# Projecting the queries first and weaving attention into the mLSTM heads of a hybrid transformer layer

## The chip, the core and the metric

The kernel runs on one core of one Trainium2 chip. Its time is the device time of one execution in microseconds (us); the time of a kernel is the median of several runs. The engines named below are TensorE (PE in the profile; its weight loads are listed apart, as PEld), VectorE (DVE), ScalarE (ACT), GpSimd (POOL) and SyncE (SP, which issues most DMAs here). TensorE writes its results to PSUM, eight banks of 2 KB on each of 128 partitions.

## What is computed

One layer of a diffusion backbone, for 128 context tokens (`xp`) and 1024 latent tokens (`xs`), model width 1024, all in float32. In the reference, cut to what matters:

```python
def trunk_layer(x, mods, ..., rope, ctx_kv, init_f, init_b):
    sh1, sc1, g1, sh2, sc2, g2 = mods                  # silu(cond) @ w_ada + b_ada
    h = rmsnorm(x, norm1_w) * (1 + sc1) + sh1
    aq, ak, av, mq, mk, mv, mo, mg = split(h @ w_in)   # 512, 128, 128, 4 x 512, 16 columns
    aq, ak = rmsnorm(aq, q_norm_w), rmsnorm(ak, k_norm_w)      # per head of 64
    # latent tokens: rotary on aq and ak, keys and values of the context cache appended
    attn_o = attention(aq, keys, vals)                 # 8 query heads, 2 key heads
    hm, st_f, st_b = mlstm_bidir(mq, mk * 128 ** -0.5, mv, gates(mg), init_f, init_b)
    hm = rmsnorm(hm, mlstm_norm_w) * sigmoid(mo)       # 4 heads of 128
    x = x + g1 * (concat([attn_o, hm]) @ w_out)        # 1024 x 1024
    h2 = rmsnorm(x, norm2_w) * (1 + sc2) + sh2
    gate, up = split(h2 @ w_gu)                        # 2 x 2816 columns
    x = x + g2 * ((silu(gate) * up) @ w_down)
```

A latent token attends to 1024 latent and 128 cached context keys, a context token to the 128 context keys alone. The mLSTM works in chunks of 128 tokens, forwards and backwards, with a 128 x 129 state per head and direction. A last rmsnorm gives `y_prompt` and `y_sample`; the context's keys, values and mLSTM states are outputs too.

## The kernel before

The 1152 tokens are nine **blocks** of 128 (block 0 is the context), and three blocks are a **chunk** (`CB`, `NCH`). Most large products are done to float32 accuracy with operands split in two float32r tiles, a rounded part `hi` and the rest `lo`: each block then needs three TensorE products (hi x hi, hi x lo, lo x hi). `load_piece` (L139) loads 128 x 1024 weights by DMA, casts them to `whi` on ScalarE (L152) and subtracts on GpSimd or VectorE (`sub`, L135) for `wlo`. The products stand in `linear_tok` (L399 to L401, tokens on the partitions), `q_group` (L670 to L672, transposed queries of an mLSTM head, 384 columns), `three_blocks` (L1008 to L1010, the FFN's second product), `out_block` (L1040 to L1042) and `products` (L1189 to L1191, the FFN's first product).

The stages in order of the program:

- *Modulation and norm 1.* `shift1` and `scale1` (L279); `normalise` (L257) squares with an accumulator (L261) and scales the rows; transposed and modulated, they become `hTh` and `hTl` (L317 to L344), six tiles of 128 x 8 x 384 float32r.
- *Keys, values, gates* of all blocks, 272 columns (L415); `evac_kvg` adds the gate bias on VectorE.
- *mLSTM heads* (L791 to L838). `head_project` of head h is woven with `head_mlstm` (the scan) of head h - 1. `weave` (L62) emits the main generator and takes steps from side generators at given rates; `beside` (L780) shares them among several. Beside heads 0 to 2 run `gate_work` (L418) and `ada_rest` (L348, the other modulations, `strip_products` of 512 columns), beside head 3 `k_work` (key norm and rotary). A head's evacuation makes `kt`, `va`, `so` and `kT` for each block (L649 to L663); the scan makes weighted values `wv` (L696), states `cs` (L709), masked scores `sd`, sums `nu` (L758) and outputs `hm` (L768 to L772), and writes one `hm_d` in DRAM (L776).
- *Queries* (L835 to L838 beside scan 3, the rest at L962 beside `key_stacks` and the first steps of `attention(0)`); they go through `q_d` in DRAM.
- *Attention* (L877), a chunk at a time: for each block and head six score products into the three-bank tile `S` (one buffer), the maximum (L920), the exponential (L921), a float16 pair `ph`, `pl` (L924, L925), transposes by DMA (L927, L928), and, for each two heads, value products into `po` (L942, L943), scaled into `oT` (L945 to L949).
- *Output projection.* `prefill` (L1045) does the mLSTM half for all blocks, `attn_out` (L1096) the attention half of a chunk, then `norm2` (L1141). Beside it `attention(1)` begins, and `gate_up_pair` (L1172) does the first two blocks' share of two FFN slices early.
- *FFN* (L1326 to L1369), a chunk at a time, with the attention of the next chunk beside it.

PSUM is first split in two pools of four banks: `wi` (L170) for projections and `mm` for all else; from L868 on `mm` has four, `po` one, `S` three. The emitted order is a first order only: the Tile scheduler (`schedule_with_timeline_sim=True`) places the instructions of each engine by its own estimate of times, and `hot(n)` (`tc.high_priority`) raises the priority of what it wraps. Each engine then works its list in order, and a waiting instruction holds up all behind it on that engine.

## Time and profile before

| | |
|---|---|
| median of 3 runs (lowest to highest) | 1618.56 us (1618.33 to 1621.84) |
| the profiled execution | 1619.03 us |
| its span, first to last instruction | 1617.1 us |
| its mean granted TensorE clock | 0.977 |
| read from and written to HBM | 181.16 MB, 11.69 MB |
| all DMA traffic, mean rate | 232.71 MB, 144 GB/s |

The profile comes from one execution, so sums from its rows are to be compared with that execution's own time. A row of the groups names a line, an engine, an operation and its tiles (out<-in), partitions x elements and type, and the count; behind the bar stand busy time, the mean of one in ns, and the engine's idle time just before these instructions, with what ended most of it. Matmuls are pipelined, so the time of a matmul's row is not the time that it takes from TensorE. The granted clock is the share of full speed that TensorE was allowed. Between 381.6 and 622.6 us, and in the first 52, there are windows at half speed.

### The profile page before, as it was taken

What the parts mean: (1) busy time and instruction counts of PE and PEld (TensorE: products, weight loads), DVE (VectorE), ACT (ScalarE), POOL (GpSimd) and SP (SyncE); (2) the same over time, 40 slices, a digit from 0 to 9 for tenths busy, and PEclk for the clock granted to TensorE, in tenths of its full rate; (3) what the DMA queues carried; (4) which work ended last, traced back from release to release, by engine and by line L of the source; (5) the groups of instructions that cost most, each with busy time, mean ns of one, the idle gap of its engine ahead of it and who ended that gap; (6) DMA issues with size and microseconds to landing.
All of it is one profiled execution on the core that took longest, in us unless ns stands there. A gap on an engine that the chain in (4) does not pass through costs nothing. (4 is left out here: it accounts for less than half of the span.)

```text
span 1617.1 us, 23358 instructions
## 1 busy us (share of the span) xinstructions
PE 1532.5 (95%) x8670; PEld 1366.1 (84%) x8670; DVE 965.3 (60%) x1969; ACT 689.8 (43%) x1193; POOL 618.0 (38%) x392
## 2 busy tenths in 40 slices
PE   6899999899898968999999999999999999999996
PEld 2888888898676757998989899898898989999995
DVE  4842363957877668577663646767674474432445
ACT  3522242424534556555643344565552453333322
POOL 1511030413345324443445344444344445544443
PEclk8999999999898988999999999999999999999998
DMA  9244443303155865777773446777684445534441
GB/s 358 67 155 125 117 142 52 82 22 71 50 183 134 180 153 116 174 181 178 180 179 113 148 153 216 188 179 175 156 185 131 131 144 176 151 127 146 144 130 65
DMA packets 386311, 232.71 MB, mean 144 GB/s; under 512 B 169910, under 2 KB 346502, under 8 KB 386198
## 3 DMA queue, kind: packets, MB, share of 16 engines
q1 hardware_dynamic: 384342, 228.04, 52.5%
q10 hardware_dynamic: 1856, 3.19, 0.6%
q8 instruction: 68, 1.11, 0.3%
q14 instruction: 45, 0.37, 0.1%
HBM read 181.16 MB, written 11.69 MB: 119 GB/s over the span
## 5 line engine op out<-in xcount | busy, mean ns | idle before, releaser
L135 POOL TENSOR_TENSOR wlo<-raw,whi 128x1024 fp32r<-128x1024 f32 (+1 forms) x159 | 390.2, 2459 | 512.3 <-ACT whi L152 474.4
L152 ACT CAST whi<-raw 128x1024 fp32r<-128x1024 f32 x239 | 245.0, 1026 | 361.7 <-DMA raw<-in_w_gu_dram 112.8
L1190 PE MATMUL mm<-aTl,whi 128*128 128x384 f32 (+2 forms) x1088 | 363.6, 334 | 0.0
L1189 PE MATMUL mm<-aTh,whi 128*128 128x384 f32 (+2 forms) x1088 | 362.5, 335 | 0.8 <-DVE tn L1217 0.8
L1191 PE MATMUL mm<-aTh,wlo 128*128 128x384 f32 (+2 forms) x1088 | 363.2, 334 | 0.0
L1189 PEld LDWEIGHTS mm<-aTh,whi 128*128 128x128 f32 x1088 | 204.5, 188 | 2.2 <-DVE tn L1217 1.4
L1190 PEld LDWEIGHTS mm<-aTl,whi 128*128 128x128 f32 x1088 | 204.9, 188 | 0.7
L1191 PEld LDWEIGHTS mm<-aTh,wlo 128*128 128x128 f32 x1088 | 204.9, 188 | 0.2
L135 DVE TENSOR_TENSOR wlo<-raw,whi 128x1024 fp32r<-128x1024 f32 (+1 forms) x80 | 98.4, 1230 | 151.7 <-ACT whi L152 147.8
L1008 PE MATMUL mm<-whi,hl 128*128 128x512 f32 x372 | 146.4, 398 | 0.8 <-ACT hl L1221 0.7
L1009 PE MATMUL mm<-wlo,hl 128*128 128x512 f32 x372 | 146.9, 396 | 0.0
L1010 PE MATMUL mm<-whi,hl 128*128 128x512 f32 x372 | 144.3, 396 | 0.8 <-POOL hl L135 0.8
L399 PE MATMUL wi<-whi,hTh 128*128 128x384 f32 (+2 forms) x392 | 135.9, 347 | 5.2 <-ACT hTh L341 5.1
L925 DVE SCALAR_TENSOR_TENSOR pl<-pr,st,ph 128x1152 f16<-128x1152 f32 (+1 forms) x72 | 111.6, 1550 | 47.7 <-ACT ph L924 47.6
L401 PE MATMUL wi<-whi,hTl 128*128 128x384 f32 (+2 forms) x392 | 133.6, 343 | 1.3 <-POOL hTl L135 1.3
L400 PE MATMUL wi<-wlo,hTh 128*128 128x384 f32 (+2 forms) x392 | 133.5, 341 | 0.0
L921 ACT ACTIVATE pr<-S,st 128x1152 f32<-128x1152 f32 (+1 forms) x72 | 81.2, 1128 | 99.7 <-DVE st L920 90.6
L135 POOL TENSOR_TENSOR hl<-tn,hl 128x384 fp32r<-128x384 f32 x66 | 83.5, 1266 | 105.0 <-ACT hl L1221 104.9
L998 DVE TENSOR_TENSOR x<-x,t 128x512 f32<-128x512 f32 x102 | 116.9, 1168 | 0.8
L1217 DVE SCALAR_TENSOR_TENSOR tn<-tn,mm 128x384 f32<-128x384 f32 (+2 forms) x68 | 36.6, 539 | 134.2 <-PE mm L1191 100.4
L918 PE MATMUL S<-kst,qT 128*128 128x384 f32 (+1 forms) x400 | 88.1, 356 | 13.9 <-ACT pr L921 13.8
L920 DVE TENSOR_REDUCE st<-S 128x1 f32<-128x1152 f32 (+1 forms) x72 | 88.8, 1233 | 20.7 <-PE S L918 20.3
(323 smaller groups left out, 2714.2 us busy)
## 6 DMA issues: line engine op xcount, KB each, us to landing
raw<-in_w_gu_dram SPq DMA_DIRECT2D x132, 512.0 KB, 4.0
raw<-in_w_down_dram SPq DMA_DIRECT2D x60, 512.0 KB, 3.6
a<-in_w_ada_dram SPq DMA_DIRECT2D x32, 512.0 KB, 4.2
gl<-g_d SPq DMA_DIRECT2D x36, 256.0 KB, 3.8
aw<-in_w_ada_dram SPq DMA_DIRECT2D x16, 512.0 KB, 8.9
raw<-in_w_in_dram SPq DMA_DIRECT2D x32, 256.0 KB, 5.6
raw<-in_w_out_dram SPq DMA_DIRECT2D x15, 512.0 KB, 4.9
x<-in_x_sample_dram SPq DMA_DIRECT2D x13, 512.0 KB, 6.4
```

What stands on the lines that cost most here:

```text
L135: (dve if eng == "dve" else pool).tensor_tensor(out=out, in0=full, in1=hi, op=ALU.subtract)
L152: nc.scalar.copy(hi[:, :n], raw[:, :n])
L399: mm(ps[:, :n], ah, wh[:, k % 2, c0 : c0 + n], start=(k == 0), stop=False)
L400: mm(ps[:, :n], ah, wl[:, k % 2, c0 : c0 + n], start=False, stop=False)
L401: mm(ps[:, :n], al, wh[:, k % 2, c0 : c0 + n], start=False, stop=(k == KD - 1))
L998: eng.tensor_tensor(out=x1[:, cs], in0=x1[:, cs], in1=t, op=ALU.add)
L1008: mm(ps, ah, wh[:, k % 2, :], start=(k == 0), stop=False)
L1009: mm(ps, ah, wl[:, k % 2, :], start=False, stop=False)
L1010: mm(ps, al, wh[:, k % 2, :], start=False, stop=(k == nk - 1))
L1189: mm(ps, wh[:, k, :], th[:, k, :], start=(k == 0), stop=False)
L1190: mm(ps, wh[:, k, :], tl[:, k, :], start=False, stop=False)
L1191: mm(ps, wl[:, k, :], th[:, k, :], start=False, stop=(k == KD - 1))
```

## The change

- **Float16 pairs for the input projection.** `hT` and the pieces of `w_in` are scaled by powers of two taken from bounds (for `hT` from `scale1` and `shift1`, for weights from the largest absolute value, found on ScalarE by `Abs` with its result thrown into PSUM banks) and split in a float16 `hi` and `lo`; the inverse scale is applied as the results are evacuated. The class `Scaled` does load, scale and pairs. There are still three products for each block.
- **Order.** The queries are projected right after keys, values and gates, with the gate work, the key work and the remaining modulations but one beside them. `attention(0)` is woven into the four heads at a tenth of a step for each unit, with its key stacks and `S` from there on. The last scan has beside it the new `attn_out_first` (the attention half of the output projection for chunk 0, its result written to `x1a_d` in DRAM), the last modulation (gate 5) and the start of `attention(1)`. `hm_d` is three tensors, one a chunk, and the last head writes `hm` in thirds.
- **Engines.** `va` and the first half of `hm` move from VectorE to ScalarE, `so` and (heads 0 to 2) `wv` from VectorE to GpSimd, `so` as two operations.
- **Output projection and FFN.** `gate_up_pair` is gone; `prefill` takes one block at a time, with `norm2` of chunk 0 one block behind.
- **Pools.** Tiles of the projection and of attention lie on the right side. In the heads PSUM has two banks for `wi`, three for `mm` and three for `S`; values use an `mm` bank until the heads are done, then `mm` has four and `po` one.

The core of the diff:

```diff
-QFIRST = [(0, 1), (2,), (3,)]
-QREST = [(4,), (5, 6), (7, 8)]
+SINGLES = [(b,) for b in range(NB)]
...
-    hm_d = drp.tile([TOK, 512], F32, name="hm_d")
+    hm_d = [drp.tile([CT, 512], F32, name=f"hm_d{c}") for c in range(NCH)]
     g_d = drp.tile([2, 2, D], F32, name="g_d")
+    x1a_d = [drp.tile([P, D], F32, name=f"x1a_d{i}") for i in range(CB)]
...
+    def power_scale(tp, one, bound, out):
+        ps = bank()
+        transpose(ps[0:1, 0:P], bound)
+        v = tp.tile([1, 4], F32, name=nm("pv"), tag="pv", bufs=2)
+        dve.tensor_reduce(out=v[:, 0:1], in_=ps[0:1, 0:P], axis=AX.X, op=ALU.max)
+        powers(v, 1)
+        yield
+        ps = bank()
+        mm(ps[:, 0:2], one, v[:, 2:4], start=True, stop=True)
+        dve.tensor_copy(out, ps[:, 0:2])
...
+    class Scaled:
+        def __init__(self, srcs, shape, raws=None):
+            self.srcs, self.shape, self.raws, self.made = srcs, shape, raws, None
+        def ready(self):
+            a, b = self.shape
+            n = self.n = a * b
+            raws = self.raws or [wp.tile([P, 1024], F32, name=nm("iraw"), tag="iraw", bufs=4) for _ in self.srcs]
+            self.raws = raws
+            for raw, src in zip(raws, self.srcs):
+                for part, ap_ in src:
+                    dma(part(raw[:, :n].rearrange("p (a b) -> p a b", b=b)), ap_)
+            yield
+            t = gp.tile([P, 20], F32, name=nm("isc"), tag="isc", bufs=3)
+            for j, raw in enumerate(raws):
+                for i in range(2):
+                    act(bank()[:, 0 : n // 2], raw[:, i * n // 2 : (i + 1) * n // 2], AF.Abs, accum_out=t[:, 12 + 2 * j + i : 13 + 2 * j + i])
+                yield
+            dve.tensor_reduce(out=t[:, 4:5], in_=t[:, 12:20], axis=AX.X, op=ALU.max)
+            dve.tensor_tensor(out=t[:, 4:5], in0=t[:, 4:5], in1=hsc[:, 3:4], op=ALU.mult)
+            yield from power_scale(gp, one1, t[:, 4:5], t[:, 6:8])
+            dve.tensor_tensor(out=t[:, 8:9], in0=t[:, 6:7], in1=hsc[:, 3:4], op=ALU.mult)
+            dve.tensor_scalar(out=t[:, 9:10], in0=t[:, 7:8], scalar1=P ** -0.5, scalar2=None, op0=ALU.mult)
+            dve.tensor_scalar(out=t[:, 10:11], in0=t[:, 7:8], scalar1=0.5, scalar2=None, op0=ALU.mult)
+            self.scale, self.inv, self.inv_k, self.inv_half = t[:, 8:9], t[:, 7:8], t[:, 9:10], t[:, 10:11]
+        def pairs(self, dve_every=2):
+            out = []
+            n, b = self.n, self.shape[1]
+            for j, raw in enumerate(self.raws):
+                w = wp.tile([P, 2, 1024], F16, name=nm("ipair"), tag="ipair", bufs=4)
+                hi, lo = w[:, 0, :n], w[:, 1, :n]
+                if j % dve_every == 0:
+                    act(hi, raw[:, :n], AF.Copy, scale=self.scale)
+                    dve.scalar_tensor_tensor(out=lo, in0=raw[:, :n], scalar=self.scale, in1=hi, op0=ALU.mult, op1=ALU.subtract)
+                else:
+                    act(raw[:, :n], raw[:, :n], AF.Copy, scale=self.scale)
+                    nc.scalar.copy(hi, raw[:, :n])
+                    sub(lo, raw[:, :n], hi, "pool")
+                out.append(tuple(v.rearrange("p (a b) -> p a b", b=b) for v in (hi, lo)))
+            return out
...
+            if b0 < 2 * CB:
+                dve.tensor_scalar(out=xs[b0 + i], in0=xs[b0 + i], scalar1=rs[:, i : i + 1], scalar2=None, op0=ALU.mult)
+            else:
+                act(xs[b0 + i], xs[b0 + i], AF.Copy, scale=rs[:, i : i + 1])
...
-    hTh = [hp.tile([P, KD, CT], F32R, name=f"hTh{c}", tag=f"b{2 * c}") for c in range(NCH)]
-    hTl = [hp.tile([P, KD, CT], F32R, name=f"hTl{c}", tag=f"b{2 * c + 1}") for c in range(NCH)]
+    hp = ctx.enter_context(tc.tile_pool(name="hpk", bufs=1, side="right", reuse_waits="tile"))
+    hT = [hTp.tile([P, 2, KD, CT], F16, name=f"hT{c}", tag=f"hT{c}") for c in range(NCH)]
+    hTh, hTl = [t[:, 0] for t in hT], [t[:, 1] for t in hT]
+    dve.tensor_reduce(out=hs2, in_=shift1, axis=AX.XY, op=ALU.max, apply_absolute_value=True)
+    dve.tensor_reduce(out=hsc[:, 0:1], in_=scale1, axis=AX.XY, op=ALU.max, apply_absolute_value=True)
+    dve.scalar_tensor_tensor(out=hsc[:, 0:1], in0=hsc[:, 0:1], scalar=float(D) ** 0.5, in1=hs2, op0=ALU.mult, op1=ALU.add)
+    powers(hsc, P)
+    for t in (scale1, shift1):
+        dve.tensor_scalar(out=t, in0=t, scalar1=hsc[:, 2:3], scalar2=None, op0=ALU.mult)
...
+            if b == 0:
+                with hot(300):
+                    emit(kvg_steps)
+                    kvg_pairs = kvg.pairs()
+            if b >= 3:
+                for _ in range(3):
+                    next(ada)
+            if b in (3, 4, 5, 6):
+                next(steps)
+            if b == 8:
+                emit(steps)
...
-            dve.tensor_copy(va[:, 0:P], ps[:, P : 2 * P])
+            act(va[:, 0:P], ps[:, P : 2 * P], AF.Copy, scale=w.inv)
             pool.memset(va[:, P : P + 1], 1.0)
             th = mlp.tile([P, P], F32, name=nm("th"), tag="th", bufs=2)
-            act(th, ps[:, 2 * P : 3 * P], AF.Tanh, scale=0.5)
+            act(th, ps[:, 2 * P : 3 * P], AF.Tanh, scale=w.inv_half)
             so = mlp.tile([P, P], F32, name=nm("so"), tag="so", bufs=MB)
-            dve.scalar_tensor_tensor(out=so, in0=th, scalar=1.0, in1=mwh[:, h * P : (h + 1) * P], op0=ALU.add, op1=ALU.mult)
+            pool.tensor_tensor(out=so, in0=th, in1=mwh[:, h * P : (h + 1) * P], op=ALU.mult)
+            pool.tensor_tensor(out=so, in0=so, in1=mwh[:, h * P : (h + 1) * P], op=ALU.add)
...
-        yield from q_group((0, 1))
-        yield from q_group((2,))
-        yield from linear_tok(pieces, P, 3 * P, evac)
+        for c in range(NCH):
+            yield from q_group((c,))
+        for i, _ in enumerate(linear_tok(pieces, P, 3 * P, evac, SINGLES)):
+            if i % 6 == 5:
+                next(nxt_steps, None)
+            yield
+        emit(nxt_steps)
...
-                dve.tensor_scalar(out=wv, in0=blocks[b][2], scalar1=qcol(1, d, b, h), scalar2=None, op0=ALU.mult)
+                if h < NH - 1:
+                    pool.tensor_tensor(out=wv, in0=blocks[b][2], in1=qcol(1, d, b, h).to_broadcast([P, P + 1]), op=ALU.mult)
+                else:
+                    dve.tensor_scalar(out=wv, in0=blocks[b][2], scalar1=qcol(1, d, b, h), scalar2=None, op0=ALU.mult)
...
+        ends = {2: 0, 5: 3, 8: 6} if h == NH - 1 else {8: 0}
...
-            dve.tensor_scalar(out=hm[:, b, :], in0=nu[:, 0, 0:P], scalar1=dn[:, 0:1], scalar2=None, op0=ALU.mult)
+            act(hm[:, b, :], nu[:, 0, 0:P], AF.Copy, scale=dn[:, 0:1])
...
+    w_q = groups_in[0].pairs()
+    steps = groups_in[1].ready()
+    next(steps)
+    weave(linear_tok(w_q, 0, 512, evac_q(qp, qcc, qss, qw)), beside((gates, 0.25), (ada, 0.8), (kwork, 0.8), (steps, 0.3)), 40, 40)
+    emit(steps)
+    groups_in[1].made = groups_in[1].pairs()
+    emit(ada)
+    emit(kwork)
+    es_r.close()
+    es_h.close()
+    es_a.close()
+    es_b.close()
+    ap = ctx.enter_context(tc.tile_pool(name="ap", bufs=1, side="right", reuse_waits="tile"))
+    ap2 = ctx.enter_context(tc.tile_pool(name="ap2", bufs=1, side="right", reuse_waits="tile"))
+    psum["S"] = ctx.enter_context(tc.tile_pool(name="pS", bufs=1, space=PSUM, reuse_waits="tile"))
+    es_d = ExitStack()
+    for name, bufs in (("wi", 2), ("mm", 3)):
+        psum[name] = es_d.enter_context(tc.tile_pool(name="p" + name, bufs=bufs, space=PSUM, reuse_waits="tile"))
...
-                            po = psum["po"].tile([P, 512], F32, name=nm("po"), tag="po")
+                            po = psum["po"].tile([P, 512], F32, name=nm("po"), tag="po") if "po" in psum else bank()
...
+        ahead = load_hm(0)
         load_x1(0)
-        ahead = load_hm(0)
-        order = [(b,) for b in range(NB - 2)] + [tuple(range(NB - 2, NB))]
-        for grp in order:
-            parts = {}
-            for b in grp:
-                load_x1(b + 1)
-                s = b % 6
-                th, tl = (t[:, s // 3 * 4 : s // 3 * 4 + 4, s % 3 * P : (s % 3 + 1) * P] for t in (ath, atl))
-                parts[b] = th, tl
-                hm, ahead = ahead, load_hm(b + 1)
-                ps = bank()
-                for j in range(4):
-                    transpose(ps[:, j * P : (j + 1) * P], hm[:, j * P : (j + 1) * P])
-                psv = ps.rearrange("p (j x) -> p j x", j=4)
-                nc.scalar.copy(th, psv)
-                sub(tl, psv, th.bitcast(F32), "dve")
+        ws = out_pieces(1)
...
+    def attn_out_first(oT, ready):
+        x1 = hTp.tile([P, CB, D], F32, name="x1a", tag="hT0")
+        gt = hTp.tile([P, 6, 512], F32, name="gta", tag="hT1")
+        mx = hTp.tile([P, CB, NQ, P], F32R, name="mxa", tag="hT2")
+        ip = [wp.tile([P, 1024], F32R if i < 2 else F32, name=nm("ip"), tag="ipair", bufs=4) for i in range(4)]
+        ir = [wp.tile([P, 1024], F32R if i < 2 else F32, name=nm("ir"), tag="iraw", bufs=4) for i in range(4)]
+        turn = [0]
...
-    def gate_up_pair(a, fs):
-        a["early"] = []
...
+    oT = []
+    done = set()
+    att = attention(0, oT, done, 200, 100)
+    weave(head_project(0, sts[0]), beside((gates, 0.3), (att, 0.1)), 96, 96)
+    emit(gates)
+    for h in range(1, NH):
+        scan = head_mlstm(h - 1, sts[h - 1])
+        weave(head_project(h, sts[h]), beside((scan, 0.67), (att, 0.11)), 96, 96)
+        emit(scan)
+    scan = head_mlstm(NH - 1, sts[NH - 1])
+    first, ada = attn_out_first(oT, done)
+    oT = []
+    att = chain(att, attention(1, oT, set()))
+    weave(scan, beside((ada, 0.35), (first, 0.25), (att, 0.1)), 57, 57)
+    while len(done) < CB:
+        next(att)
+    emit(first)
+    emit(ada)
+    emit(scan)
+    es1.close()
+    es_wp.close()
+    es_d.close()
+    for name, bufs in (("mm", 4), ("po", 1)):
+        psum[name] = ctx.enter_context(tc.tile_pool(name="q" + name, bufs=bufs, space=PSUM, reuse_waits="tile"))
+    wp = ctx.enter_context(tc.tile_pool(name="wp", bufs=1, reuse_waits="tile"))
+    hp = ctx.enter_context(tc.tile_pool(name="hp", bufs=1, reuse_waits="tile"))
...
+    for _ in prefill(cur, nxt):
+        due += 0.35
         while due >= 1.0:
+            next(att, None)
```

442 lines of the change are left out of this document (211 added, 231 removed).

## The prediction

> **What bounds the kernel now.** I read the page's engine table first, then busy time by stage (the page's slices are too coarse, so I cut the span where TensorE's main products change), then matmul spacing in the timeline, then TensorE's waits in the worst stage.
>
> ```profile
> span 1617.1 us, 23358 instructions
> PE 1532.5 (95%) x8670; PEld 1366.1 (84%) x8670; DVE 965.3 (60%) x1969; ACT 689.8 (43%) x1193; POOL 618.0 (38%) x392
> ```
>
> TensorE (PE) is the bound, but 95% overstates it: a matmul's row lasts longer than its slot. The slot is the distance between starts in a dense stretch, from the timeline:
>
> ```profile
> 1454.74 0.34 PE L1190 MATMUL mm<-aTl,whi 128*128 128x384 f32 x1
> ...
> 1460.98 0.34 PE L1190 MATMUL mm<-aTl,whi 128*128 128x384 f32 x1
> ...
> 881.66 0.39 PE L1010 MATMUL mm<-whi,hl 128*128 128x512 f32 x1
> ...
> 884.45 0.39 PE L1010 MATMUL mm<-whi,hl 128*128 128x512 f32 x1
> ...
> 737.17 0.28 PE L943 MATMUL po<-plT,vs 128*128 128x256 f16 x1
> ...
> 737.83 0.27 PE L943 MATMUL po<-plT,vs 128*128 128x256 f16 x1
> ```
>
> The first two rows are 36 matmuls apart: 6.24 / 36 = 0.173 us for 384 columns of float32r (a row says 0.34). The next two are 12 apart: 0.232 us for 512 columns. The last two are 6 apart: 0.110 us for 256 columns of float16 (0.109 over longer stretches). Count times slot I call TensorE's **work**. By stage (columns: start:end, length, then busy time and instructions of PE, PEld, DVE, ACT, POOL, granted clock, DMA share, GB/s):
>
> ```profile
> 0.00:34.20 34.20, 21.36 (x108) 7.53 (x108) 10.40 (x44) 8.76 (x16) 3.44 (x9) 0.90 0.96 352
> 34.20:81.80 47.60, 40.90 (x280) 38.30 (x281) 42.73 (x114) 28.32 (x65) 27.33 (x22) 0.89 0.35 116
> 81.80:148.80 67.00, 67.00 (x411) 54.25 (x410) 23.09 (x77) 16.46 (x42) 8.69 (x12) 1.00 0.46 139
> 148.80:227.00 78.20, 78.20 (x541) 69.74 (x540) 30.84 (x109) 23.89 (x77) 8.21 (x15) 1.00 0.44 120
> 227.00:308.20 81.20, 78.69 (x523) 70.03 (x523) 52.58 (x175) 25.22 (x90) 20.44 (x31) 1.00 0.35 80
> 308.20:381.60 73.40, 68.72 (x439) 66.16 (x438) 48.70 (x164) 23.57 (x85) 20.27 (x28) 1.00 0.16 44
> 381.60:468.80 87.20, 77.59 (x383) 62.15 (x381) 69.06 (x237) 38.72 (x104) 32.37 (x30) 0.94 0.33 76
> 468.80:622.60 153.80, 124.56 (x603) 99.60 (x603) 114.06 (x214) 81.25 (x124) 57.13 (x35) 0.88 0.69 164
> 622.60:1603.50 980.90, 974.66 (x5393) 897.99 (x5392) 564.42 (x800) 439.44 (x586) 438.91 (x215) 1.00 0.58 156
> 1603.50:1617.10 13.60, 0.80 (x4) 0.32 (x2) 9.46 (x42) 4.22 (x9) 1.26 (x1) 0.67 0.31 116
> ```
>
> They are: loads and first modulations; k/v/gates projection (DVE busy 42.7 of 47.6, so VectorE sets it); heads 0 to 3; queries beside scan 3; attention of chunk 0 with the output projection; FFN; tail. The stage 468.8 to 622.6, worked out:
>
> ```profile
> L1040 PE MATMUL mm<-whi,aTh 128*128 128x512 f32 x72 | 30.0, 420 | 2.5 <-ACT aTh L1076 1.5 <-DVE rv L125 0.9
> L918 PE MATMUL S<-kst,qT 128*128 128x384 f32 x114 | 29.7, 406 | 11.5 <-ACT pr L921 11.5
> L942 PE MATMUL po<-phT,vs 128*128 128x256 f16 x75 | 20.1, 300 | 11.3 <-DVE oT L947 4.8 <-DMA phT<-ph 4.5 <-ACT whi L152 1.6
> ```
>
> Out products (L1040 to L1042 with all their operands) 268 x 0.232 = 62; scores 114 x 0.173 + 10 small = 20; values (L942, L943) 150 x 0.109 = 16; transposes and rest 9: 108 us of work in 153.8. 46 us are lost, partly in waits (the row of L918: scores wait for the exponential of the head before, since the S tile has one buffer), partly because the granted clock was 0.88 (0.12 x 153.8 = 18 us). The same sum for the other stages gives, as work in time: 13 in 34, 36 in 48, 58 in 67, 71 in 78, 73 in 81, 66 in 73, 69 in 87, FFN and tail 971 in 994. In all 1465 of 1617: **152 us are slack**, 65 of it in the two stages from 381.6 to 622.6. There the change can win.
>
> **The change part by part.**
>
> *Float16 pairs.* Three products per block stay three; only the slot shrinks. No row has a 384-column float16 matmul; 256 columns in 0.109 us is 2.35 columns a ns, so I take 0.1635, 0.218 and 0.116 us for 384, 512 and 272 columns, against 0.173, 0.232 and 0.126 (bounds: no gain, and twice this gain, should some ns of the 0.109 be a fixed cost of a matmul). 1152 x 0.0095 + 216 x 0.014 + 216 x 0.010 = 16.1 us off the work.
>
> ```profile
> L399 PEld LDWEIGHTS wi<-whi,hTh 128*128 128x128 f32 x392 | 75.0, 191 | 12.7 <-ACT hTh L341 5.8 <-issue 4.6 <-ACT th L656 0.4
> L942 PEld LDWEIGHTS <-vs 128*128 128x128 f16 x292 | 29.1, 100 | 26.0 <-issue 9.5 <-DVE oT L947 6.1 <-DMA phT<-ph 5.9
> ```
>
> Weight loads fall from 191 to 100 ns. They run beside the products (a 191 ns load fits into a 173 ns slot only so), hence I count nothing for them. The Trainium skill, page "TensorE: Matmul & The Clock Gate", section "Part 3: Packing small matmuls", says otherwise: a weight load overlaps running matmuls only where the row group differs, and these loads take all rows. By that rule 1584 x 0.091 = 144 us would go (an estimate); it is the last rival, and the 0.173 us slot speaks against it.
>
> *FFN without the early pair.* 96 products of 256 columns and 96 of 128 become 96 of 384.
>
> ```profile
> 645.54 0.28 PE L1189 MATMUL mm<-aTh,whi 128*128 128x128 f32 x1
> ...
> 646.54 0.27 PE L1190 MATMUL mm<-aTl,whi 128*128 128x128 f32 x1
> ```
>
> Nine slots, so 128 columns take 0.111. 256 lie between that and 0.173; I take 0.118, the float16 slot plus a little: 96 x (0.118 + 0.111 - 0.173) = 5.4 us off (bounds 4.7 and 10.7). *Scaling.* Six scale chains add 12 small matmuls at 0.11: 1.3 us. Work: 1465 - 16.1 - 5.4 + 1.3, some **1445 us**.
>
> *Other engines.* In the instruction order of the changed kernel, up to the first FFN product:
>
> ```profile
> L261 ACT ACTIVATE jk<-x 128x1024 bf16<-128x1024 f32 x9 | 9.5, 1056 | 1.4 <-DMA x<-in_x_sample_dram 0.9 <-DMA x<-in_x_prompt_dram 0.2
> L261 ACT ACTIVATION_READ_ACCUMULATOR jk<-x 128x1 f32 x9 | 1.7, 190 | 0.0
> L921 ACT ACTIVATE pr<-S,st 128x1152 f32<-128x1152 f32 x64 | 78.3, 1223 | 90.2 <-DVE st L920 86.0 <-DVE rv L125 2.1 <-DVE pl L925 1.8
> L920 DVE TENSOR_REDUCE st<-S 128x1 f32<-128x1152 f32 x64 | 86.5, 1351 | 17.9 <-PE S L918 17.5
> L925 DVE SCALAR_TENSOR_TENSOR pl<-pr,st,ph 128x1152 f16<-128x1152 f32 x64 | 105.3, 1645 | 47.1 <-ACT ph L924 47.0
> L658 DVE SCALAR_TENSOR_TENSOR so<-th,mwh 128x128 f32<-128x128 f32 x36 | 11.8, 330 | 10.6 <-POOL hm L772 9.7 <-ACT th L656 0.3
> L696 DVE TENSOR_SCALAR wv<-va,QT 128x129 f32<-128x129 f32 x64 | 25.9, 409 | 37.7 <-PE mm L705 36.5 <-issue 0.9
> L772 POOL TENSOR_TENSOR hm<-hm,so 128x128 f32<-128x128 f32 x36 | 17.3, 482 | 57.3 <-ACT jkh L771 54.1 <-issue 2.2 <-POOL va L654 1.0
> ```
>
> ScalarE gains 48 absolute-value passes (half of 1.06 us, plus 0.19 for the accumulator, 0.7 each: 34 us), ten casts more for the pairs (10), 36 `va` and 36 `hm` evacuations (0.33 each, 24) and nine attention heads (1.22 for the exponential, as much for the copy and 0.19: 24): 92 more, some 340 in all. VectorE gives away 108 operations like `so` and 48 `wv`: 108 x 0.33 + 48 x 0.41 = 55 us, but takes twelve halves of pairs (1.3 each), nine attention heads (1.35 + 1.65 each) and the scale chains: 420, as before. POOL gains 120 products at 0.48: 240. None comes near 600, so these engines bound single stages only.
>
> *By stage of the new order* (work counted from that order; time is my estimate):
>
> - Loads to first k/v/gates product: 14 of work. The scale of `hT` hangs a dozen VectorE operations of 0.15 us behind `scale1`: 36 (was 34).
> - k/v/gates: 40. VectorE was busy 10.4 + 42.7 = 53 us up to the end of this stage; the new order puts 15 us more ahead of the last gate evacuation (scale chains, three more subtractions, nine modulation units, pieces of the k work). It was saturated, so 12 of them are paid: 60 (was 48).
> - Queries with gates, k work, modulation: 57 of work, 62 of VectorE: 64.
> - Heads 0, 1, 2: 51, 72, 72. Heads 0 to 3 ran at 87 to 90%; VectorE has 27, 50, 45 us there and ScalarE 35 to 50, so there is room for one attention head every 9 us, whose chain of scores, maximum and exponential (1.04 + 1.35 + 1.22 + 0.19) needs 3.8. I keep 90%: 57, 80, 81.
> - Head 3 and the last scan, with the first out products, gate 5 and the start of attention 1: 85 at 90% is 95, then 42 in 57: there VectorE has 60, and the scan's tail was the slow part of stage 381.6 to 468.8 (69 in 87).
> - Other half of the output projection, norm2 and more of attention 1: 70 in 82, with some 6 us until the first w_out pieces are there, since they take the place of tiles that the first half still reads.
>
> Sum: 36 + 60 + 64 + 57 + 80 + 81 + 152 + 82 = **612** against 622.6, though 504 of work stand before the first FFN product instead of 494: nine attention heads of chunk 1 have moved ahead of it. FFN and tail: 1445 - 504 = 941 of work and 21 of slack (23 before, less a little, since chunk 0's FFN has fewer attention heads beside it), **962**. Span 1574; the profiled execution takes 1619.03 for a span of 1617.1, 1.9 more, and the median, 1618.56, is 0.5 below it. So **1575 us**.
>
> **Rivals.**
>
> - *Better fill.* Attention fills the scans' gaps as it does in the FFN (971 in 994, 97%). Heads and scans: 322 / 0.97 = 332 instead of 370: **1537**. For it: the FFN does it with the same attention beside it. Against: in heads 0 and 1 TensorE's row shows no gap (78.20 of 78.20), yet its work is 90% of that; slots beside other kinds of product are longer, and attention adds more of these.
> - *Float16 isn't faster.* Slots stay 0.173 and 0.232, so 1575 + 16: **1591**. Only values at 256 columns speak for the gain.
> - *Slower: PSUM banks.* In the heads `mm` has three banks instead of four, projections two instead of four, and `mm` now also takes the values (18 products, 2.0 us, and their evacuation), query transposes and eight scratch outputs of the absolute value per head. TensorE issues in order, so one late bank holds all.
>
> ```profile
> L758 DVE TENSOR_TENSOR nu<-mm,it 128x258 f32<-128x258 f32 x32 | 13.4, 420 | 10.4 <-PE mm L755 9.7 <-ACT it L751 0.7
> L947 DVE SCALAR_TENSOR_TENSOR oT<-po,vsc,ol 64x128 f32<-64x128 f32 x72 | 24.5, 341 | 14.7 <-ACT ol L945 13.1
> ```
>
> If each of the 27 scan banks of a head waits for one evacuation of 0.42, each scratch 0.7 and each of five value tiles three evacuations of 0.34, that is 11 + 6 + 5 = 22 us a head, 88 in all; less the 18 that the 90% holds already, **1645**. It turns the result from 11 us a head on (1619).
> - *Loads don't overlap*: 1575 + 16 - 144 = **1447**, if all of it shows.
>
> **How the numbers follow.** My stages 0.45 (1555 to 1600); better fill 0.22; float16 no faster, or slower stages yet still a gain, 0.14; PSUM banks 0.14; within 0.2% of before 0.03 (about what a measurement can tell from no change); loads 0.02. The range 1530 to 1620 leaves out most of the bank case and the loads. Faster 0.83, same 0.03, slower 0.14.
>
> **What would show it.** Right: projection slots near 0.1635 us; last k/v/gates product near 96, queries done near 160, first FFN product near 612; clock 1.00 in the heads; FFN and tail near 962. Wrong: waits of projections for ScalarE or of `mm` products for `isc` and `ol` in the heads (banks); slots of 0.173; VectorE idle while TensorE waits before 160.

## The result, and the profile after

The changed kernel takes **1624.6 us** (median of 20 runs, 1618.87 to 1628.66), the kernel before, run beside it, 1619.61 (20 runs). The ratio is 1.0026, with a 95% interval of 1.0016 to 1.0037: slower by a quarter of a per cent, where 1575 us were forecast. The profiled execution took 1626.38 us. Its page, first lines:

```profile
span 1624.6 us, 23438 instructions
...
PE 1507.5 (93%) x8592; PEld 1254.6 (77%) x8592; DVE 937.6 (58%) x1895; ACT 755.6 (47%) x1373; POOL 657.5 (40%) x507
```

Busy time by stage, cut at the same products as before (same columns as in the prediction): loads; keys, values and gates; queries; heads 0, 1, 2; head 3 up to the first out product; the rest of the last scan; output projection and norm 2; FFN; tail.

```profile
0.00:40.00 40.00, 22.95 (x111) 8.72 (x112) 13.31 (x67) 13.86 (x36) 2.56 (x9) 0.84 0.97 355
40.00:93.70 53.70, 47.63 (x384) 32.92 (x384) 42.45 (x138) 36.17 (x84) 19.52 (x18) 0.90 0.59 186
93.70:170.30 76.60, 65.44 (x368) 30.02 (x368) 57.67 (x161) 39.10 (x67) 31.70 (x23) 0.96 0.50 150
170.30:228.50 58.20, 54.70 (x328) 33.74 (x326) 33.37 (x108) 26.95 (x78) 19.73 (x32) 0.94 0.17 49
228.50:309.50 81.00, 75.05 (x490) 54.00 (x489) 48.35 (x119) 54.11 (x143) 25.89 (x48) 1.00 0.36 74
309.50:387.70 78.20, 74.93 (x511) 54.19 (x509) 41.63 (x119) 45.04 (x133) 26.00 (x54) 1.00 0.40 68
387.70:494.50 106.80, 94.42 (x628) 69.38 (x628) 65.18 (x170) 54.43 (x146) 40.01 (x70) 0.92 0.53 116
494.50:547.00 52.50, 44.62 (x255) 34.63 (x254) 42.90 (x110) 29.07 (x71) 14.39 (x14) 0.97 0.53 135
547.00:653.70 106.70, 82.40 (x407) 65.56 (x406) 62.54 (x144) 47.81 (x76) 43.53 (x31) 0.90 0.59 159
653.70:1611.10 957.40, 944.97 (x5123) 871.42 (x5122) 520.89 (x725) 404.82 (x536) 432.95 (x211) 1.00 0.58 156
1611.10:1624.60 13.50, 0.38 (x2) 0.00 (x0) 9.28 (x42) 4.22 (x9) 1.26 (x1) 0.61 0.30 117
```

Set against the forecast, with TensorE's work (count times slot, small products by the distance of their own rows, one count for all kernels from here on; slack is length less work):

| part | forecast | measured | work | slack |
|---|---|---|---|---|
| loads | 36 | 40.0 | 9 | 31 |
| keys, values, gates | 60 | 53.7 | 38 | 15 |
| queries | 64 | 76.6 | 56 | 21 |
| heads 0, 1, 2 | 57, 80, 81 | 58.2, 81.0, 78.2 | 194 | 23 |
| head 3 and last scan | 152 | 159.3 | 122 | 37 |
| up to the first FFN product | 82 | 106.7 | 73 | 33 |
| FFN and tail | 962 | 970.9 | 939 | 32 |

By this count the work fell from 1453 to 1432 us, 21 less (forecast: 20). The slack rose from 164 to 193, where I let it fall by 23. Before the first FFN product it went from 138 to 161 us, and the FFN with its tail added 6.

### The profile page after: what moved, and what is told of

The parts are those of the page before. It is cut to its first block, busy times and chain, and to the rows that moved or that the text cites. A ratio compares the mean times of both kernels' runs of the same rounds, so it can differ in the third digit from the quotient of the medians.

```text
span 1624.6 us, 23438 instructions
## 1 busy us (share of the span) xinstructions
PE 1507.5 (93%) x8592; PEld 1254.6 (77%) x8592; DVE 937.6 (58%) x1895; ACT 755.6 (47%) x1373; POOL 657.5 (40%) x507
## 3 DMA queue, kind: packets, MB, share of 16 engines
q1 hardware_dynamic: 385110, 231.84, 53.7%
## 5 line engine op out<-in xcount | busy, mean ns | idle before, releaser
L136 POOL TENSOR_TENSOR wlo<-raw,whi 128x1024 fp32r<-128x1024 f32 (+1 forms) x144 | 352.0, 2448 | 419.3 <-ACT whi L153 387.9
L153 ACT CAST whi<-raw 128x1024 fp32r<-128x1024 f32 (+1 forms) x216 | 221.6, 1026 | 403.9 <-DMA raw<-in_w_gu_dram 160.4
L1305 PE MATMUL mm<-aTl,whi 128*128 128x384 f32 x1056 | 355.1, 336 | 0.0
L1304 PE MATMUL mm<-aTh,whi 128*128 128x384 f32 x1056 | 354.0, 336 | 0.9 <-DVE tn L1323 0.9
L1306 PE MATMUL mm<-aTh,wlo 128*128 128x384 f32 x1056 | 354.6, 336 | 0.0
L1306 PEld LDWEIGHTS mm<-aTh,wlo 128*128 128x128 f32 x1056 | 198.4, 188 | 1.5 <-issue 1.3
L136 DVE TENSOR_TENSOR wlo<-raw,whi 128x1024 fp32r<-128x1024 f32 (+1 forms) x72 | 85.9, 1193 | 157.0 <-ACT whi L153 156.8
L514 PE MATMUL wi<-ipair,hT 128*128 128x384 f16 (+2 forms) x432 | 142.6, 332 | 9.8 <-ACT ipair L217 3.6
L515 PE MATMUL wi<-ipair,hT 128*128 128x384 f16 (+2 forms) x432 | 143.4, 332 | 4.3 <-DVE ipair L218 4.3
L516 PE MATMUL wi<-ipair,hT 128*128 128x384 f16 (+2 forms) x432 | 143.3, 332 | 0.2 <-POOL hT L136 0.2
L1323 DVE SCALAR_TENSOR_TENSOR tn<-tn,mm 128x384 f32<-128x384 f32 x66 | 36.4, 551 | 134.5 <-PE mm L1306 95.6
L1030 ACT ACTIVATE ph<-pr,st 128x1152 f16<-128x1152 f32 (+1 forms) x72 | 83.8, 1164 | 28.0 <-issue 8.1
```

Source lines behind the costliest of these rows:

```text
L136: (dve if eng == "dve" else pool).tensor_tensor(out=out, in0=full, in1=hi, op=ALU.subtract)
L153: nc.scalar.copy(hi[:, :n], raw[:, :n])
L514: mm(ps[:, :n], ah, wh[:, k % 2, c0 : c0 + n], start=(k == 0), stop=False)
L515: mm(ps[:, :n], ah, wl[:, k % 2, c0 : c0 + n], start=False, stop=False)
L516: mm(ps[:, :n], al, wh[:, k % 2, c0 : c0 + n], start=False, stop=(k == KD - 1))
L1304: mm(ps, wh[:, k, :], th[:, k, :], start=(k == 0), stop=False)
```

## The experiments

Theory after the result: the smaller slots are a gain, and the new order and the scaling give it back in waits, at the queries and around the last scan. Rival: the heads lose it, to PSUM banks shared with attention. Each ratio is to the kernel before, run on the same chip (the changed kernel: 1.0026). A ratio is that of medians, while stages and waits are read from one execution of each kernel; the executions of the changed kernel alone spread over 10 us, so a few us between the stages of two kernels prove little. The code is shortened.

### The float16 pairs alone (f16_alone)

The kernel before, with `hT` and the pieces of `w_in` in float16, unscaled:

```diff
-hi = wp.tile([P, 1024], F32R, ...); hTh = hp.tile([P, KD, CT], F32R, ...)
+hi = wp.tile([P, 2048], F16, ...);  hTh = hp.tile([P, 2, KD, CT], F16, ...)[:, 0]
```

> The kernel before with one part of the change alone: hT and the pieces of w_in as float16 pairs (hi and lo, without the scaling), order, pools and engines as before. The slots of the changed kernel (0.1625, 0.216, 0.116 us for 384, 512, 272 columns) give 18 us less work than before. Theory (the smaller slots are a gain, and the new order gives it back): 1599 to 1606 us, ratio 0.988 to 0.992. Rival (the slots gain nothing where other engines set the pace, so the new order is neutral): within 4 us of before, ratio 0.998 to 1.002.

Measured: 1611.29 us, ratio 0.9957 (0.9942 to 0.9972), less than the theory's gain. The first FFN product starts at 605.0 us instead of 622.6: the whole 17.6 are there. The FFN and tail then take 1004.5 instead of 994.5 for the same work of 969. TensorE's longest waits from the first FFN product on, before and then in this run (sum, times, longest):

```profile
PE S L918 <- ACT pr L921: 1.7, 1, 1.7
PE po L942 <- DMA phT<-ph: 1.1, 2, 0.8
```

```profile
PE po L943 <- DMA phT<-ph: 3.5, 3, 2.6
PE po L944 <- DMA plT<-pl: 1.6, 1, 1.6
```

Value products wait for transposed probabilities 5.1 us instead of 1.3. The pairs gain what their slots say, and 10 of the 17.6 us are lost in the FFN, whose code is the same. These waits are 4 of the 10; the rest is spread over smaller ones and not taken apart.

### The scaling (fixed, nopass, abs_sbuf, abs_dve)

In `fixed` a constant takes the place of the weights' bound; `nopass` leaves out only the passes; `abs_sbuf` moves their thrown-away result; `abs_dve` moves the passes to VectorE:

```diff
-act(bank()[:, 0 : n // 2], raw[...], AF.Abs, accum_out=t[...])   # and maximum, transpose, powers, broadcast
+dve.memset(t[:, 4:5], 2.0 ** -6); powers(t[:, 4:8], P)                          # fixed
+dve.memset(t[:, 12:20], 0.125)                                   # nopass, the chain stays
+act(gp.tile([P, 512], BF16, ...), raw[...], AF.Abs, accum_out=t[...])           # abs_sbuf
+dve.tensor_reduce(out=t[:, 12 + j : 13 + j], in_=raw[:, :n], op=ALU.max, ...)   # abs_dve
```

> The changed kernel with a constant bound for the weights' scales: the absolute-value passes on ScalarE (with their PSUM banks), the maximum, its transpose and its broadcast over partitions are left out. Theory (the scale chains cost a few us at the start and in the queries stage and are hidden in the heads): 4 to 9 us faster than the changed kernel, ratio 0.997 to 1.000. Rival (the chains and the banks that they take hold up every head): 15 us or more faster, ratio at or below 0.993.

> The changed kernel without the absolute-value passes of the weights alone (the partial maxima are constants); the chain behind them (maximum, transpose, powers, broadcast by a product) stays. The constant scale of the run fixed took both away and was 17 us faster than the changed kernel. If the 48 passes on ScalarE and the mm banks that they take are the cost: 10 us or more of the 17 come back, ratio at or below 0.997. If the chain is the cost: within 5 us of the changed kernel, ratio 1.000 to 1.004.

> The changed kernel with the thrown-away result of the absolute-value passes written to one small SBUF tile instead of mm banks. If the banks (eight more per head in a pool of three, TensorE behind them in order) are what the passes cost: 8 us or more faster than the changed kernel, ratio at or below 0.998. If it is ScalarE's time, in order ahead of evacuations: no gain, ratio 1.001 to 1.005.

> The changed kernel with the weights' absolute maximum taken on VectorE (24 reductions of some 1.1 us over whole pieces) instead of 48 passes on ScalarE (37 us by their rows). If ScalarE's order, ahead of evacuations, is what the passes cost: 5 us or more of the 12 that nopass gained come back, ratio 0.996 to 0.9995. If VectorE is as tight in these stages: ratio 1.001 or above.

Measured: fixed 1607.21 us, 0.9932 (0.9910 to 0.9954); nopass 0.9954 (0.9938 to 0.9970); abs_sbuf 1.0011 (0.9993 to 1.0029); abs_dve 0.9993 (0.9978 to 1.0008). Against the changed kernel these are 15, 12, 2 and 5 us less. The passes' rows in the changed kernel:

```profile
L200 ACT ACTIVATE mm<-iraw 128x512 f32<-128x512 f32 x40 | 24.1, 604 | 4.6 <-DVE cs L823 3.8 <-DMA iraw<-in_w_in_dram 0.6
L200 ACT ACTIVATION_READ_ACCUMULATOR mm<-iraw 128x1 f32 x40 | 8.0, 199 | 0.0
L200 ACT ACTIVATE mm<-kraw 128x272 f32<-128x272 f32 x8 | 3.1, 388 | 1.0 <-DMA kraw<-in_w_in_dram 1.0
L200 ACT ACTIVATION_READ_ACCUMULATOR mm<-kraw 128x1 f32 x8 | 1.5, 188 | 0.0
```

That is 37 us of ScalarE, near the 34 that I counted, but I let it cost nothing. A third of it comes out as time, though ScalarE is busy 47% of the span. Of the 12 us, 5 come back when the passes move to VectorE, which frees ScalarE and the banks together; the banks by themselves are worth 2, within what the interval leaves open. That the passes stand in ScalarE's list ahead of evacuations is only argued: TensorE's waits for `th`, the evacuation there, fall from 3.7 us to 2.4 both in nopass and in abs_dve, and all its waits from the first product of keys, values and gates to the first FFN product add up to 74 us in the changed kernel, 70 in nopass and 74 in abs_dve. The scaling costs 15 us in all, close to what the rival of fixed said and far from its theory, and twice the 7 that the pairs alone gained at the end. (The passes add up absolute values, so the scale follows a bound, not the largest value itself, as the part on the change says; only abs_dve takes that.)

What is left when the scaling goes is small. `fixed` and `f16_alone` were run beside the same runs of the kernel before, and take 1607.21 and 1611.29 us: all the rest of the change (order, engines, pools, output projection, no early pair) is worth some 4 us, and the runs of the two overlap. I had put 28 of the 44 us on it.

### The queries' norm (qplain)

```diff
-norm_rope(qp, cc, ss, qr[:, 0:nb], nb, NQ, qw, ...)
```

> The changed kernel without norm and rotary of the queries (left out: they go to attention as projected). Theory (VectorE's chains set the pace of the new queries stage, 74 us from its first to its last product with 56 of work): that stretch shrinks to 60 to 66 us and the whole by 8 to 14 us against the changed kernel, ratio 0.994 to 0.998. Rival (weights, modulation loads and key work set it): under 4 us, ratio 1.000 to 1.004.

This kernel leaves out norm and rotary of the queries, so only its time means anything. Measured: 0.9963 (0.9948 to 0.9978), 10 us less than the changed kernel, as the theory said, but in another place: the stretch from first to last product takes 70.3 us, not 60 to 66. The queries stage of this run:

```profile
92.50:164.60 72.10, 64.41 (x369) 30.01 (x369) 36.29 (x106) 35.92 (x63) 19.60 (x17) 0.95 0.55 169
```

VectorE fell from 57.7 to 36.3 us and the stage only from 76.6 to 72.1; head 0 behind it went from 58.2 to 51.4. So VectorE's norm doesn't set the queries stage alone; it runs over into head 0. Without the absolute-value passes (nopass) the products of this stage took 65.0 from first to last instead of 73.6: so at least two chains keep it at 77, and neither alone.

### Attention in the heads, and the banks (noweave, noweave6, psum32, psum14)

```diff
-weave(head_project(h, sts[h]), beside((scan, 0.67), (att, 0.11)), 96, 96)
+weave(head_project(h, sts[h]), beside((scan, 0.67)), 96, 96)                    # noweave; noweave6 with mm 6, S later
-for name, bufs in (("wi", 2), ("mm", 3)):
+for name, bufs in (("wi", 3), ("mm", 2)):                                       # psum32; psum14: 1 and 4
```

> The changed kernel without attention beside heads 0 to 3 (both rates taken out), so that all of attention 0 stands beside and behind the last scan. Theory (the heads have little slack, attention in them costs its own work, some 2 us a head, but saves the chain of 4 us a head elsewhere): stages of heads 0 to 2 become some 10 to 25 us shorter in sum, the part from the last scan to the first FFN product 30 to 60 longer, ratio 1.015 to 1.03. Rival (PSUM banks shared with attention slow the heads by far more than attention's own work): heads 0 to 2 become over 40 us shorter, ratio at or below 1.002.

> The run noweave (no attention beside the heads) with six mm banks in the heads instead of three: attention's score tile is opened only behind the heads. In noweave the heads 0 to 2 took 50.9, 68.0 and 68.4 us. Bank rival: the scan's products wait for banks, so these three become 15 us or more shorter in sum, ratio at or below 1.046. Theory (three banks are enough without attention's values and transposes): under 8 us shorter, ratio 1.051 to 1.058.

> The changed kernel with three PSUM banks for the projections and two for all else in the heads, instead of two and three. The prediction's bank rival (every scan product, value tile and transpose waits for the evacuation of its bank) makes 20 us or more of losing the third mm bank: ratio 1.015 or above. Theory (the stages of heads 0 to 2 came out at 58, 81 and 78 us, as forecast without bank waits): within 8 us of the changed kernel, ratio 0.998 to 1.008.

> The changed kernel with one bank for the projections and four for all else in the heads. Bank rival: heads faster, ratio at or below 0.996. Theory: no gain from the fourth mm bank; with one projection bank each block's evacuation stands between its products and the next block's, 36 times some 1 us and 12 times 0.5, so slower: ratio 1.01 to 1.03.

Measured: noweave 1710.36 us, 1.0569 (1.0550 to 1.0588), far beyond the theory's range. Heads 0 to 2 took 50.8, 68.0 and 68.4, 30 less in sum, and 20 of these are work that left. But from head 3 on to the first FFN product 384 us pass instead of 266. TensorE's longest waits there:

```profile
PE mm L1048 <- DMA phT<-ph: 33.7, 9, 8.0
PE S L1024 <- ACT pr L1027: 27.3, 10, 3.7
```

With nothing beside it an attention head waits for its exponential and for its transposes; the granted clock was 0.68 from 421 to 601 us. So the weave is worth 88 us to this order. It costs the heads 10 us of slack beyond attention's own work.

noweave6: heads 0 to 2 took 51.9, 65.1 and 69.1, 1 us less in sum, so three banks are enough there without attention. Its ratio, 1.0498 (1.0458 to 1.0538), is below the range that I gave the theory; the 11 us came behind the heads. psum32 is 1.0383 (1.0357 to 1.0409): the third `mm` bank is worth 58 us, as the bank rival has it, and the theory falls. In its profile 18 of them lie in heads 0 to 2, 28 in head 3 up to the first out product and 10 in the rest of the last scan. psum14 is 1.0158 (1.0140 to 1.0176): a fourth one doesn't pay for a lost projection bank. TensorE's longest wait in its heads:

```profile
PE mm L115 <- ACT kt L751: 11.0, 16, 1.7
```

With one bank for projections TensorE waits 16 times for `kt` to be evacuated. With attention in the heads, a fourth `mm` bank beside two for projections could not be tried: `S` holds three of the eight. So the bank rival is a cliff one bank away; with three banks heads 0 to 2 came out as forecast.

### The last scan (rates, c0act)

```diff
-weave(scan, beside((ada, 0.35), (first, 0.25), (att, 0.1)), 57, 57)
+weave(scan, beside((ada, 0.35), (first, 0.5), (att, 0.3)), 57, 57)              # rates
-dma(c0[:, 0:P], I["state_C"][0, 0, d, h])
+(nc.scalar.dma_start if h == NH - 1 else dma)(c0[:, 0:P], I["state_C"][0, 0, d, h])   # c0act
```

> The changed kernel with more beside the last scan: output projection at 0.5 of a step per unit instead of 0.25, attention at 0.3 instead of 0.1. Theory (from 467 to 494 us TensorE has 10 us of gaps and half clock since products that are ready stand behind the scan in its list): first out product 8 to 15 us earlier, first FFN product 3 to 8 earlier, ratio 0.998 to 1.001. Rival (the scan's own chain of states, with its loads behind the modulation's in SyncE's queue, sets this part): no gain, ratio 1.002 to 1.005.

> The changed kernel with the last head's first states loaded from ScalarE's queue instead of SyncE's, where the second direction's load stands behind loads of w_ada that wait for TensorE (issued at 483, landed near 493). Theory (that queue delays the last scan): first out product 5 to 8 us earlier than 494.5, ratio 0.999 to 1.001. Rival (the scan's chain of states is what is slow, loads come in time for it): no change, ratio 1.002 to 1.004.

Measured: rates 1.0068 (1.0043 to 1.0094). The first out product came at 481.5 instead of 494.5, as the theory had it, and the first FFN product at 667.0 instead of 653.7. Of TensorE's waits in between:

```profile
PE mm L323 <- DMA ip<-in_w_ada_dram: 6.2, 3, 5.0
PE po L1048 <- DMA phT<-ph: 5.2, 1, 5.2
```

Modulation's loads and attention's transposes share SyncE's queue, and with more attention beside the scan TensorE waits for both; that the shared queue is the reason was not tested. The ratio lies above both ranges. c0act: 1.0034 (1.0020 to 1.0048), first out product at 500.5: the theory of the late state load falls.

### The joint behind the last scan (joint, att1late, joint3, joint6)

In the changed kernel the scan's last product is at 547 us, and 17 of the next 33 us are slack. SyncE's queue there:

```profile
547.66 1.29 SPq L152 DMA_DIRECT2D raw<-in_w_out_dram  x2
549.05 1.88 SPq L1033 DMA_TRANSPOSE phT<-ph  x1
551.02 4.23 SPq L1034 DMA_TRANSPOSE plT<-pl  x1
555.36 2.30 SPq L152 DMA_DIRECT2D raw<-in_w_out_dram  x2
557.71 0.46 SPq L1150 DMA_DIRECT2D t<-hm_d  x1
```

```diff
-dma(hm, hm_d[...])
+(nc.scalar.dma_start if b < 2 else dma)(hm, hm_d[...])           # joint; x1 likewise
-att = chain(att, attention(1, oT, set()))
+att = attention(1, oT, set())                                    # att1late: only behind the scan, one step later
-hm = t2(); raw = wp.tile(..., tag="raw", bufs=2)
+hm = ap.tile(..., tag="qr"); raw = ap2.tile(..., tag="pr")       # joint3, on att1late: block 0, first two pieces
-th, tl = t[:, 0:4], t[:, 4:8]
+th, tl = mix_spare if b == 0 else (t[:, 0:4], t[:, 4:8])         # joint6, on joint3; last hm writes by pool.dma_start
```

> The changed kernel, with the first two loads of hm and of x1 in the prefill issued from ScalarE's queue instead of SyncE's, where they stand behind attention's DMA transposes and the w_out pieces. Theory (the 8.6 us in which TensorE waits for hm at 555, and the half clock behind it, are made by SyncE's queue): the wait falls to under 2 us, first FFN product 6 to 10 us earlier, ratio 0.996 to 0.999 of before. Rival (DMA bandwidth, 277 GB/s from 547 to 580, sets the hole): the wait moves to the w_out pieces and the time stays at ratio 1.002 to 1.004.

> The changed kernel with attention 1 begun only after the first steps of the prefill, not beside the last scan, so that no DMA transposes stand in SyncE's queue ahead of hm at the joint behind the scan. Theory (that queue makes the hole: transposes that wait for TensorE's value products, then the w_out pieces, then hm): the wait of 8.6 us for hm falls to 4 or less; five attention heads move behind it, so the first FFN product comes 10 to 16 us earlier and the FFN takes 8 to 10 longer; ratio 0.998 to 1.001. Rival (the joint is made by w_out's loads and casts, two raw tiles at a time): the wait stays over 6 us, ratio 1.002 to 1.005.

> The run att1late with two more edits at the joint behind the last scan: the first hm is loaded into the attention's free query tile and the first two w_out pieces into its two free probability tiles, which are not memory that the scan holds, so that these loads are issued before the scan ends. In att1late TensorE waits 17.3 us for hm there (four w_out loads, two raw tiles at a time, stand ahead of it on SyncE's queue). Theory (memory and queue order make the joint): the wait falls under 9 us and the first FFN product comes 6 to 10 us earlier, ratio 0.993 to 0.996 of before. Rival (bandwidth, 282 to 398 GB/s there, makes it): wait over 14 us, ratio 0.998 to 1.000.

> The run joint3 with three more edits at the joint: block 0's mx in a spare piece of the key tiles, which the scan does not hold, at high priority, and the last head's hm written from GpSimd's queue instead of ScalarE's. In joint3 the wait for hm was gone, and TensorE waited 15.3 us for the cast of mx instead, which stood on ScalarE's list behind the issue of hm's last write (that waits for the scan's last root and product) and behind the cast of a w_gu piece. Theory (the joint is a row of in-order waits, each covering the next): the wait for mx falls under 4 us, 5.6 us of products move ahead, the wait for the second hm or for x grows to 5 to 10, and the first FFN product comes 2 to 6 us earlier, ratio 0.995 to 0.998. Rival (the later loads set the joint whatever comes first): first FFN product within 1 us of joint3, ratio 0.998 to 1.000.

Measured: joint 1.0066 (1.0047 to 1.0085), att1late 0.9990 (0.9978 to 1.0001), joint3 0.9987 (0.9971 to 1.0003), joint6 1.0030 (1.0014 to 1.0047). TensorE's longest wait at the joint, first in the changed kernel, then in that order (one fence for each kernel):

```profile
PE mm L115 <- DMA t<-hm_d: 8.6, 1, 8.6
```

```profile
PE mm L115 <- DMA t<-hm_d: 15.7, 1, 15.7
```

```profile
PE mm L115 <- DMA t<-hm_d: 17.3, 1, 17.3
```

```profile
PE mm L1136 <- ACT mx L1173: 15.9, 2, 15.3
```

```profile
PE mm L115 <- DMA t<-hm_d: 12.0, 1, 12.0
```

joint and att1late aimed at the wait for hm and made it longer; joint3 removed it, joint6 cut the wait for `mx` to 4.2 us, and in both the next wait took its place. On ScalarE's queue (joint) hm stood behind the cast of a `w_out` piece that waited for its own load. Without attention's transposes (att1late) it stood behind four loads of `w_out` with two raw tiles to hold them; SyncE's queue there:

```profile
531.87 9.46 SPq L152 DMA_DIRECT2D raw<-in_w_out_dram  x4
541.37 0.46 SPq L1150 DMA_DIRECT2D t<-hm_d  x1
```

In joint3 hm was loaded at 521, before the scan ended, and the cast of `mx` was late instead. ScalarE's list there:

```profile
546.32 1.04 ACT L153 CAST whi<-raw 128x1024 fp32r<-128x1024 f32 x1 [4.34 <-DMA raw<-in_w_gu_dram]
548.02 0.38 ACTq L889 DMA_DIRECT2D hm_d<-hm  x1
548.44 0.58 ACT L1173 CAST mx<-mm 128x512 fp32r<-128x512 f32 x1 [1.08 <-POOL hm L887]
```

The issue of hm's last write waits for GpSimd's product, that for a root on VectorE, and the cast behind it. In joint6 block 0's products run at 537, and the second hm is late. So one queue doesn't make the joint. I read it as a row of in-order waits, each covering the next, but no run shows that by a gain: from the scan's last product to the first FFN product the changed kernel, joint, att1late, joint3 and joint6 have 33, 41, 39, 36 and 36 us of slack.

Bandwidth, the rival of joint and joint3, is not ruled out. joint3's numbers are the rival's: a wait over 14 us, a ratio of 0.9987, and a first FFN product at 640.8 us, no earlier than att1late's 640.9. Against the rival, the DMA engines were busy only 56% in these 15 us, at 171 GB/s. For it, part of each wait for hm is the load itself, behind the pieces of `w_out` issued before it. In the changed kernel it is issued at 557.71 and TensorE goes on at 564.12, 6.4 us later, the DMA engines 80% busy; in joint, att1late and joint6 it takes 7.3, 6.6 and 7.5 us, at 89% and more. joint3's early load of the same size landed 2.7 us after its issue. So some 4 to 5 us of each wait for hm may be bandwidth, and the rest stands before the issue.

joint6 reached its first FFN product 5.4 us before joint3, as expected, but its ratio is above both ranges: its FFN took 8.6 longer with 5 more work in it. What att1late gained, 6 us, doesn't show at the joint: its FFN has 10.6 of slack instead of 18.8, a difference that a new order makes elsewhere too, and its first out product came at 485.3 instead of 494.5 (4 of these 9 us were there when head 3 began).

### Both together (combo, combo2)

> The edits of fixed (constant bound for the scales) and joint3 together. If their gains add (15 us of fixed against the changed kernel, 6 of att1late, 6 to 10 of joint3): 1592 to 1600 us, ratio 0.983 to 0.988, faster than the kernel before and the changed one. If they overlap: ratio 0.990 to 0.993.

> The edits of joint6 with the constant bound of fixed. If a shorter joint adds to fixed: ratio 0.985 to 0.990 of before. If not: 0.990 to 0.993, as fixed and combo.

Measured: combo 1605.41 us, 0.9915 (0.9885 to 0.9944); combo2 0.9954 (0.9937 to 0.9970). The gains overlap: combo's interval holds the ratio of fixed, and combo2 is above both of its ranges. Both beat the two kernels, as do fixed, nopass and f16_alone; the best, combo, is 0.85% under the kernel before, with a constant bound in place of one found from the weights.

## Why the prediction was wrong, point by point

The span came out 50.6 us over the forecast of 1574. By the rows of the table above that is 4.0 in the loads, 6.3 less in keys, values and gates, 12.6 in the queries, 0.6 less in heads 0 to 2, 7.3 in head 3 and the last scan, 24.7 up to the first FFN product, and 8.9 in the FFN and tail.

- **Float16 slots: right.** I took 0.1635, 0.218 and 0.116 us. In the changed kernel's timeline these two rows are 24 products apart, so 3.90 / 24 = 0.1625:

```profile
201.66 0.33 PE L515 MATMUL wi<-ipair,hT 128*128 128x384 f16 x1
...
205.56 0.33 PE L515 MATMUL wi<-ipair,hT 128*128 128x384 f16 x1
```

  512 and 272 columns have 0.216 and 0.116. The 17.6 us of f16_alone before the FFN are these slots and no more. The rival in which weight loads don't overlap, from the Trainium skill, page "TensorE: Matmul & The Clock Gate", section "Part 3: Packing small matmuls", is refuted here: the loads fell to 99 ns each, and only the slots' gain appeared.
- **Work: right; heads: right with luck.** Work fell by 21 (20 forecast); heads 0 to 2 took 217.4 (218 forecast). But my 90% held no cost of the scaling, and without it (fixed) the heads take 208.9: two misses of some 9 us cancel.
- **Scaling: mis-sized.** "ScalarE gains 48 absolute-value passes" at 34 us, and "None comes near 600, so these engines bound single stages only": fixed puts the scaling at 15 us. Twelve us of VectorE in the keys' stage, scale chains among them, were charged; that stage was even 6 shorter than forecast. (VectorE's 420 us "as before" is a slip: the rows ahead of the first FFN product add up to 391 before, and to 407 now. Nothing hangs on it.) Against fixed, the changed kernel loses 6 us up to the first query product, 2 in the queries, 5 and 6 in heads 0 and 1 and 7 in the FFN, and wins some back between.
- **Queries 64: wrong, 76.6.** I set a stage of 57 of work and 62 of VectorE at little over the larger. VectorE had 58, and still 77 passed; qplain and nopass each take a part of it away, neither the whole.
- **Head 3 and last scan 152: 159.3.** The old scan had the queries' products beside it, ready at any time. Its new company is out products and modulation. The loss lies ahead of the first out product, 106.8 us where 95 were forecast, with a granted clock of 0.69 from 467.5 to 494.5. From 467.5 to 547 TensorE waits 4.6 us for `wv`, 2.9 for `cs` and 2.1 for `nu`, all VectorE's in the scan, and 3.1 for loads of `w_ada`. That the missing queries are the reason is argued; no run puts them back.
- **"Other half of the output projection ... 70 in 82, with some 6 us until the first w_out pieces are there": wrong, 106.7.** This is the largest miss, 25 us, and the step on which the forecast fell. The joint costs 17 us, not 6, and behind it 57 of work took 74. I had read the old stage's 46 lost us as attention's waits and the clock, and let them go with attention. Attention's waits did go: TensorE's for `S` and `po` fell from 25.7 us to 4.0. Others took their place, those for hm, the output projection's casts and norm 2. Before (468.8 to 622.6), then after (547 to 653.7):

```profile
PE S L918 <- ACT pr L921: 12.2, 7, 2.9
PE mm L1040 <- ACT aTh L1076: 1.5, 2, 0.8
PE mm L114 <- DMA t<-hm_d: 0.8, 1, 0.8
```

```profile
PE mm L115 <- DMA t<-hm_d: 8.6, 1, 8.6
PE mm L1136 <- ACT mx L1173: 4.2, 4, 1.8
PE mm L1138 <- DVE mx L136: 3.4, 2, 2.3
PE mm L115 <- ACT y L1283: 3.1, 1, 3.1
PE S L1024 <- ACT pr L1027: 0.4, 1, 0.4
```

  What sets the joint's 17 stays open between the row of in-order waits and busy DMA engines, since joint, att1late, joint3 and joint6 moved the waits and left the slack; what makes the 16 behind it is only read from these waits, and no run takes it apart.
- **FFN 962: 970.9**, within what a new order does to it: with one work of 938.6 its slack was 11.2 to 18.8 us in nine of the kernels run here.
- **Sign.** I had the chance of slower at 0.14 by PSUM banks. Slower it was, with the heads as forecast and some 2 us for the banks that the scaling takes. (The 18 us that I took off that rival as held by the 90% don't come out of my stages: 57 + 80 + 81 + 95 less 51, 72, 72 and 85 is 33, so its time should read 1630.) The case that came, "slower stages" beside a full float16 gain, had been given a gain by construction: I laid the slack of the old stages at attention's door, and asked no further what would fill it.

What stays open: how the 15 us of scaling divide between ScalarE's order and the scheduler's new placement behind it, what a fourth `mm` bank would bring with attention in the heads, and what the moves between engines and the new output projection are worth: they have no run of their own.

## What to carry to other kernels

Slack doesn't leave a stage with the work that waited there: here attention's waits went, others came, and 33 us stayed. Before forecasting that it goes, name the waits that remain, and what fills them once the filler is gone. Don't price passes at nothing because their engine is half idle: here 37 us of them on an engine busy 47% cost 12. And where a scheduler lays the order, an edit shifts all that follows it: here by up to 9 us of 1600 in the FFN alone, which belongs into any range.

## What the runs showed of the hardware

Tiny VectorE operations stretch beside GpSimd's long ones. In joint3, VectorE and then GpSimd:

```profile
540.67 1.87 DVE L126 TENSOR_SCALAR rv<-ssh 128x3 f32<-128x3 f32 x1 [0.47 <-ACT jkh L880]
...
542.99 2.26 DVE L128 TENSOR_SCALAR ry<-rh 128x3 int32<-128x3 int32 x1
```

```profile
540.17 2.35 POOL L136 TENSOR_TENSOR wlo<-raw,whi 128x1024 fp32r<-128x1024 f32 x1
...
542.89 2.34 POOL L136 TENSOR_TENSOR wlo<-raw,whi 128x1024 fp32r<-128x1024 f32 x1
```

Two operations on three columns end when GpSimd's subtraction ends, 1.87 and 2.26 us after their start; others of the same chain took 0.16. This root stood in the joint's chain. In joint3's whole trace, of VectorE's operations on one to nine columns, 30 took over 0.4 us: every one began inside a GpSimd operation and ended within 0.06 us of its end. None of the 510 that began outside one took over 0.23. But 73 more began inside one and stayed under 0.4, and what tells them apart isn't shown.
